# Weight units at other places within their SBUF slots, in a four-stage trunk on one core

## The chip, the core and the metric

The kernel runs on one core of one Trainium2 chip. What counts is the time on the device, in microseconds: the median of several runs of the whole kernel. Beside it stands one profiled execution, from which all durations of single instructions come.

## What is computed

One layer pair of a diffusion backbone, over 512 latent tokens and 256 context tokens of width 1024. Layer 0 is a hybrid mixer (neighbourhood attention beside spatial gating), layer 1 a retention in both directions; each is followed by a gated MLP with a depthwise convolution of width 3. Norms, and shifts, scales and gates made from a conditioning vector, lie around every part. Cut to what the change touches:

```python
q, k, v, u, g = jnp.split(h_lat @ w_in, splits, axis=-1)        # layer 0, hybrid
...
q, k, v, g = jnp.split(h_lat @ w_in, splits, axis=-1)           # layer 1, retention
kc, vc = jnp.split(h_ctx @ w_in[:, RET_QK_WIDTH:2 * RET_QK_WIDTH + RET_V_WIDTH], [RET_QK_WIDTH], axis=-1)
...
def conv_ffn(h, w_in, conv_w, conv_b, w_out):                   # both layers, D_FF = 2816
    a = dwconv3(h @ w_in, conv_w, conv_b)
    gate, up = jnp.split(a, 2, axis=-1)
    return (jax.nn.silu(gate) * up) @ w_out
```

## The kernel before

**Numbers in two parts.** Every product is made of float32 matrices that are split into a high part, rounded to the matmul's type fp32r, and the rest. `split` (lines 171 and 172) makes the high part on ScalarE and the rest on VectorE. `mm3` (lines 216 to 218) then needs three matmuls: high times high, high times low, low times high. `product` (whose calls show up as line 215 where they accumulate onto an open group) runs twelve of them over four slices of 128.

**Weight units.** Weights come in units of 128 x 1024 floats: a load into a ring of three raw tiles (`raw_unit`), then the split into a slot that holds both parts. `place` (line 185 on) gives slot `w0` to `w2` from the pool that lasts the whole kernel, and `w3` upward from the pool of a stage. A slot is either 2048 words wide, exactly two parts, or SLOT = 2112 words, 64 more. In the wide ones the two parts begin at word `at`, and `at` is any number up to 64:

```python
return [t[:, at + 1024 * x : at + 1024 * x + 1024] for x in range(2)]
```

64 words are 256 bytes. In the built program all wide slots, and the activations that meet them in matmuls (`h0`, `h1`, `hb`, `hs` and `blk`), begin at a multiple of 256 bytes, so `at` alone says how far a unit's start is from such a multiple. The high and the low part of a unit have the same remainder, since they are 4096 bytes apart.

**Which operand is which.** A matmul has one operand that is loaded into the array ahead (128 columns) and one that moves past it (256, 384 or 512 columns here). In the attention's projections (`project_pair`: wq, wk, wv), in the retention's queries and keys (`qk`: rwq, rwk) and in both MLPs' up-projections (wa, wb, wc, wd) the weights are loaded and the activations move. In the retention's values and gates (`nat`: rwv, rwg) the weights move and the activations are loaded.

**Places before.** The constants are Q1 = 16 and Q3 = 48 words. Attention projections, retention queries and keys lie at 0; values and gates at Q3; the MLPs' units at Q1, in the function `slot` of `ffn`. The second MLP's two further slots `w3` and `w4` are 2048 words wide and get their offset from gaps in the list of the stage's tiles (`order`, line 1511): 16 words ahead of `w3`, and 48 + 16 more ahead of `w4`, whose start is so also 16 words past a multiple of 64. The spatial gating's units, the output projections and the down-projections have places of their own, which stay.

**Stages.** `sgu` and `attention` (layer 0's mixer), `ffn(0)`, `retention`, `ffn(1)`. In the MLPs the hidden width is walked in 22 blocks of 128. The first two are made plainly; for the other twenty a scheme that saves products forms sums of halves of the weights and of the activations: units wa (rows 11 and 12), wb (s2, s3), wc (q3, q4) and wd (22), the last in a place of its own. A ring hands out the slots: `w2`, `w0`, `w1` in the first MLP, so wa is always in `w2`, wb in `w0`, wc in `w1`; `w0`, `w1`, `w3`, `w4` in the second, where three units per block rotate through four slots.

**Order.** The instructions of each engine stand in an order that is written out in a packed table (ORDER), which `queue` enforces. The DMA loads of weights are issued by the SP queue, each behind the one ahead of it.

Of the kernel before, what the change touches and what calls it, by code (L numbers as in the profile page):

```python
# [18 lines left out]
P = 128  # L19
# [16 lines left out]
EARLY = 2  # L36
SLOT = 2112
Q1, Q3 = 16, 48
MLP_PIECES = (
    ((0, (4, 5), 0, False), (0, (0,), 256, True), (1, (1,), 0, False), (1, (2,), 128, False), (1, (3,), 256, True)),  # L40
    ((0, (0,), 0, False), (0, (1,), 128, True), (1, (2,), 0, False), (1, (3,), 128, True)),
# [97 lines left out]
class Trunk:  # L139
# [563 lines left out]
    def finisher(self, gates, src, ab, name, xts, last=False, mlp=None):  # L703
# [23 lines left out]
        def third(r):  # L727
# [9 lines left out]
            else:  # L737
                for half, toks, c0, end in MLP_PIECES[mlp]:
                    if t in toks and all(u in done for u in toks):
# [239 lines left out]

    def project_pair(self, j, pr):  # L980

        w = [self.unit(self.a["hyb_qkv"][(4 * i + j) * P : (4 * i + j + 1) * P], f"w{'qkv'[i]}{j}") for i in range(3)]

        def lat(i):
            pr["qkv"[i]] = self.ps(f"p{'qkv'[i]}{j}", "A")
            self.proj_t(pr["qkv"[i]], w[i], 0)

        def con(i):
            if i == 0:
                pr["x"] = self.ps(f"px{j}", "A", (P, 2, 256))  # L990
            if i == 2:
                pr["y"] = self.ps(f"py{j}", "A")
            self.proj_t(pr["y"][:, :256] if i == 2 else pr["x"][:, i, :], w[i], 1)

        return [lambda f=f, i=i: f(i) for i in range(3) for f in (lat, con)]
# [177 lines left out]
    def retention(self, y, final):  # L1173
        S, V, T, G, a = self.S, self.V, self.T, self.G, self.a
        KS = float(np.float32(P) ** np.float32(-0.5))
        with ExitStack() as ctx:
            rp = self.phase(ctx, "retp", 3, SLOT)
            order = [("dist", ND), ("cos", 512), ("sin", 512), ("dec", 16), ("gng", 16), (None, 24)]
# [13 lines left out]
            gng = rp.tile([P, 16], F32, name="gng", tag="gng")  # L1192
            self.load(gng, a["gn_col"])
            w8 = lambda w: [x.rearrange("p (k c) -> p k c", k=4) for x in w]
            qk = lambda h, o, n: self.unit(a["ret_qk"][(o + h) * P : (o + h + 1) * P], f"rw{n}{h}")
            vg1 = lambda h, o, n, i, dst=None: w8(
                self.unit(a["ret_vg"][(o + h * 2 + i) * P : (o + h * 2 + i + 1) * P], f"rw{n}{h}{i}", dst, Q3)
            )
            vg = lambda h, o, n: [vg1(h, o, n, i) for i in range(2)]
            hd = [{} for _ in range(8)]  # L1200
# [180 lines left out]
            def gated(h):  # L1381
                d = hd[h]
                if h == 7:
                    gt = [x.rearrange("p (f c) -> p f c", f=2) for x in self.slot("gt7")]
                else:
                    gt = [rp.tile([P, 2, 512], F32R, name=f"gt{i}{h}", tag=f"gt{i}", bufs=1) for i in range(2)]
                for f in range(2):
                    pt = self.ps(f"rt{h}{f}", "A")
                    for t in range(4):
                        T.transpose(pt[:, t * P : (t + 1) * P], d["og"][t][:, f * P : (f + 1) * P], self.ident)  # L1390
                    gc = gng[:, 2 * h + f : 2 * h + f + 1]
                    S.activation(gt[0][:, f, :], pt, AF.Copy, scale=gc)
                    V.scalar_tensor_tensor(
                        out=gt[1][:, f, :],
                        in0=pt,
                        scalar=gc,
                        in1=gt[0][:, f, :].bitcast(F32),
                        op0=ALU.mult,
                        op1=ALU.subtract,
                    )  # L1400
                return [(gt[0][:, f, :], gt[1][:, f, :]) for f in range(2)]
# [6 lines left out]
            for h in range(8):  # L1408
# [35 lines left out]
                else:  # L1444
# [6 lines left out]
                    f = gated(h - 1)  # L1451
# [37 lines left out]
    def ffn(self, l, y, final, gates=None):  # L1489
# [4 lines left out]
        S, V, T, G, a = self.S, self.V, self.T, self.G, self.a  # L1494
        first = l == 0
        toks = (4, 5, 0, 1, 2, 3) if first else (0, 1, 2, 3)
        n = self.bn
        W = 770 if first else 512
# [4 lines left out]
        with ExitStack() as ctx:  # L1503
            fp = self.phase(ctx, f"ffnp{l}", 0)
            off = 62 if first else 0
            if first:
                order = [("blk", 9216), ("pre0", 2 * W), ("cv", 2 * W), ("cw", 176), ("yp", 1024)]
                order += [("g0", W + off, 3), ("g1", W + off, 3), ("rawu", 1024)]
            else:
                order = [("rawu", 1024), ("w5", 2048), ("w6", 2048), ("pre0", 1024), ("pre1", 1024), ("blk", 4096), ("cv", 1024)]  # L1510
                order += [(None, 16), ("w3", 2048), (None, 48), ("g0", W, 4), ("g1", W, 4), (None, 16), ("w4", 2048)]
                order += [("cw", 176), ("yp", 2048)]
            self.lay(fp, order)
            cw = fp.tile([P, 44, 4], F32, name=f"cw{l}", tag="cw")
# [11 lines left out]
                "o": ("y0", "y4", "y2") if first else ("w2", "w5", "w6"),  # L1526
            }

            def slot(kind, name, at=Q1):

                h = homes[kind][ring[kind] % len(homes[kind])]
                ring[kind] += 1
                if h == "fp":
                    return [fp.tile([P, 1024], F32R, name=f"{name}{x}", tag=tag) for x, tag in zip("hl", ("rawu", "yp"))]
                i = int(h[1])
                if h[0] == "w":
                    return self.place(i, name, at)
                pool = self.bp if i < 4 else self.lp
                return [pool.tile([P, 1024], F32R, name=f"{name}{x}", tag=f"y{i + m}", bufs=1) for m, x in enumerate("hl")]
# [63 lines left out]
            def weights(j):  # L1603
# [4 lines left out]
                def one():  # L1608
                    st["g"], st["u"] = win(j, 0), win(j, 1)
                    u = slot("i", f"wa{j}")  # L1610
                    self.split(u[0], u[1], st["g"])
                    d[11], d[12] = halves(u)

                def two():
                    u = slot("i", f"wb{j}")
                    g, up = st["g"], st["u"]
                    st["s"] = self.t2k(f"s2{j}"), self.t2k(f"s3{j}")
                    V.tensor_tensor(out=st["s"][0], in0=up[:, H[0]], in1=up[:, H[1]], op=ALU.subtract)
                    V.tensor_tensor(out=st["s"][1], in0=g[:, H[0]], in1=up[:, H[0]], op=ALU.subtract)
                    d["s", 2], d["s", 3] = halves(u)  # L1620
                    for x, v in zip((2, 3), st["s"]):
                        self.split(*d["s", x], v)
                    if soon:
                        up_half()

                def three():
                    u = slot("i", f"wc{j}")
                    q3, q4 = self.t2k(f"q3{j}"), self.t2k(f"q4{j}")
                    V.tensor_tensor(out=q3, in0=st["s"][0], in1=st["g"][:, H[0]], op=ALU.subtract)
                    V.tensor_tensor(out=q4, in0=q3, in1=st["g"][:, H[1]], op=ALU.add)  # L1630
                    d["q", 3], d["q", 4] = halves(u)
                    for x, v in ((3, q3), (4, q4)):
                        self.split(*d["q", x], v)
# [412 lines left out]
```

## Time and profile before

| what | value |
|---|---|
| median of 3 runs | 1786.02 us (1785.51 to 1786.25) |
| span of the profiled execution | 1784.0 us |
| instructions in it | 28774 |
| TensorE matmuls, and as many weight loads | 11024 |
| HBM read and written | 191.80 MB and 39.85 MB |
| DMA, mean over the span | 142 GB/s |

A row of the tables of the profile names a line of the kernel, an engine (PE is TensorE's matmuls, PEld its weight loads, DVE VectorE, ACT ScalarE, POOL GpSimd, SPq the SP queue), an operation, the tiles as output<-inputs without their numbers, and a shape. Matmuls overlap: the next starts before the last is through, so the length of one matmul is longer than the time from its start to the next start, and it is this time from start to start that adds up to the span.

### The profile page before, as it was taken

Reading aid. Unit: us, or ns where it says so; the run is one execution under the profiler, and the core shown is the slowest. Engines: PE = TensorE matmul, PEld = TensorE weight load, DVE = VectorE, ACT = ScalarE, POOL = GpSimd, SP = SyncE. Lnnn points to the kernel's source line nnn. Section 1 sums busy time; section 2 is a strip of 40 time slices with the busy share of each in tenths; the row PEclk is TensorE's granted clock in tenths of the full one; section 3 lists DMA queues with packets and bytes.
Section 4 is the critical chain, followed back from the end, with each engine's and each line's share of the span. In section 5 each row is a group of like instructions: output and inputs, shape, how many; then the busy total and the mean of one; then the engine's idle time right before and its main releaser. Section 6 shows DMA issues by size and latency. Waiting matters only on the chain.

```text
span 1784.0 us, 28774 instructions
## 1 busy us (share of the span) xinstructions
PE 1748.3 (98%) x11024; PEld 1578.7 (88%) x11024; DVE 1388.2 (78%) x2363; ACT 1017.5 (57%) x1882; POOL 340.1 (19%) x462
## 2 busy tenths in 40 slices
PE   7999999999999999999999999999999999999997
PEld 4898888799998999999899998998999789999996
DVE  3887886898887787889867666666655799998887
ACT  6633567776555555655665434433444577766773
POOL 1101322230132322222221001101001200222221
PEclk9999999999999999999999999999999999999999
DMA  8345331364687877886734332332322235887764
GB/s 304 116 133 165 99 110 45 106 180 118 171 174 174 173 174 155 164 178 161 257 126 125 118 113 71 119 95 81 97 71 60 107 122 147 214 216 185 180 145 130
DMA packets 84398, 253.44 MB, mean 142 GB/s; under 512 B 11026, under 2 KB 11538, under 8 KB 84260
## 3 DMA queue, kind: packets, MB, share of 16 engines
q1 hardware_dynamic: 55044, 191.27, 33.7%
q0 software_dynamic: 26912, 51.95, 17.1%
q10 hardware_dynamic: 2304, 8.39, 1.2%
q8 instruction: 86, 1.41, 0.3%
q14 instruction: 52, 0.43, 0.1%
HBM read 191.80 MB, written 39.85 MB: 130 GB/s over the span
## 4 chain that ended last, share of the span: by engine, by line
PE 89%; DVE 5%; ACT 3%; DMA 1%; issue 1%; POOL 1%; SPq 0%; DVEq 0%; POOLq 0%; ACTq 0%
PE px L215 11%; PE wf L216 4%; PE wf L217 4%; PE wf L218 4%; PE rn L217 4%; PE rn L216 4%; PE rn L218 4%; PE py L215 4%; PE px L216 2%; PE px L217 2%; PE px L218 2%; PE py L218 1%; PE py L217 1%; PE py L216 1%; PE ug L216 1%; PE ug L217 1%
## 5 line engine op out<-in xcount | busy, mean ns | idle before, releaser
L326 DVE SCALAR_TENSOR_TENSOR acc<-ar,cs,acc 128x512 f32<-128x512 f32 x256 | 190.5, 758 | 11.1 <-DMA ar<-in_adaw 4.3
L216 PE MATMUL rn<-rwv,h0c 128*128 128x256 f32 x384 | 107.8, 281 | 0.0
L217 PE MATMUL rn<-rwv,h0c 128*128 128x256 f32 x384 | 107.5, 281 | 0.0
L218 PE MATMUL rn<-rwv,h1c 128*128 128x256 f32 x384 | 107.2, 280 | 0.0
L1734 POOL DMA_DIRECT2D yf<-yp x64 | 56.0, 963 | 265.1 <-ACT yp L1730 237.7
L1574 ACT ACTIVATE pre<-px 128x256 f32<-128x256 f32 (+2 forms) x160 | 56.0, 369 | 78.0 <-PE px L215 55.9
L1587 DVE SCALAR_TENSOR_TENSOR cv<-pre,cw,cv 128x769 f32<-128x769 f32 (+1 forms) x88 | 77.3, 882 | 27.5 <-ACT cv L1586 26.9
L1586 ACT ACTIVATE cv<-pre,cw 128x770 f32<-128x770 f32 (+1 forms) x88 | 80.9, 925 | 21.5 <-DVE g L172 11.4
L1730 ACT COPY yp<-wf 128x512 f32<-128x512 f32 x118 | 68.4, 584 | 41.8 <-PE wf L218 34.2
L215 PE MATMUL px<-blk,wb 128*128 128x384 f32 (+1 forms) x480 | 79.2, 309 | 1.1 <-ACT pre L1574 1.1
L215 PE MATMUL px<-hs,wc 128*128 128x384 f32 (+1 forms) x480 | 78.9, 309 | 1.0 <-ACT pre L1574 0.8
L1590 DVE SCALAR_TENSOR_TENSOR cv<-pre,cw,cv 128x769 f32<-128x769 f32 (+1 forms) x88 | 76.8, 881 | 0.9
L215 PEld LDWEIGHTS px<-hs,wc 128*128 128x128 f32 x480 | 73.5, 188 | 4.1 <-ACT pre L1574 1.6
L215 PEld LDWEIGHTS px<-blk,wb 128*128 128x128 f32 x480 | 72.8, 188 | 3.8 <-ACT pre L1574 1.6
L171 ACT ACTIVATE wc<-q 128x512 fp32r<-128x512 f32 x80 | 49.8, 629 | 44.1 <-PE py L215 20.7
L216 PEld LDWEIGHTS rn<-rwv,h0c 128*128 128x128 f32 x384 | 72.4, 189 | 1.2 <-issue 0.2
L218 PEld LDWEIGHTS rn<-rwv,h1c 128*128 128x128 f32 x384 | 72.5, 189 | 0.7
L217 PEld LDWEIGHTS rn<-rwv,h0c 128*128 128x128 f32 x384 | 72.4, 188 | 0.9
L1734 POOL DMA_DIRECT2D yd<-ypg x48 | 48.4, 1053 | 122.1 <-ACT ypg L1730 104.6
L218 PE MATMUL rn<-rwg,h1c 128*128 128x256 f32 x256 | 71.3, 279 | 0.0
L217 PE MATMUL rn<-rwg,h0c 128*128 128x256 f32 x256 | 71.1, 279 | 0.0
L216 PE MATMUL rn<-rwg,h0c 128*128 128x256 f32 x256 | 71.1, 279 | 0.0
(1545 smaller groups left out, 6328.4 us busy)
## 6 DMA issues: line engine op xcount, KB each, us to landing
ar<-in_adaw SPq DMA_DIRECT2D x96, 512.0 KB
yf<-yp POOLq DMA_DIRECT2D x64, 256.0 KB, 4.3
yd<-yp POOLq DMA_DIRECT2D x54, 256.0 KB, 5.5
yd<-ypg POOLq DMA_DIRECT2D x54, 256.0 KB, 5.5
fin<-xd SPq DMA_DIRECT2D x8, 512.0 KB
xn<-in_x SPq DMA_DIRECT2D x6, 512.0 KB
xb<-in_x SPq DMA_DIRECT2D x6, 512.0 KB
xd<-xb ACTq DMA_DIRECT2D x6, 512.0 KB
```

The lines of the kernel that those rows point to most:

```text
L171: self.S.activation(hi, src, AF.Copy)
L215: mm = lambda *p, **k: self.T.matmul(*p, skip_group_check=True, **k)
L216: mm(out, lhs[0], rhs[0], start=first, stop=False)
L217: mm(out, lhs[0], rhs[1], start=False, stop=False)
L218: mm(out, lhs[1], rhs[0], start=False, stop=last)
L326: V.scalar_tensor_tensor(out=acc[s], in0=raw[:, kk * 512 : kk * 512 + 512], scalar=self.cs[:, 8 * s + k : 8 * s + k + 1], in1=acc[s], op0= ...
L1574: S.activation(pre[:, i, c : c + w], ps[:, b : b + w], AF.Copy, scale=scale)
L1586: S.activation(d, s, AF.Identity, scale=w1, bias=b)
L1587: V.scalar_tensor_tensor(out=d[:, 1:W], in0=s[:, 0 : W - 1], scalar=w0, in1=d[:, 1:W], op0=ALU.mult, op1=ALU.add)
L1590: V.scalar_tensor_tensor(out=d[:, 0 : W - 1], in0=s[:, 1:W], scalar=w2, in1=d[:, 0 : W - 1], op0=ALU.mult, op1=ALU.add)
L1730: S.copy(v, ps)
L1734: G.dma_start((yd[t] if first else y[t])[:, o], v, accum_op=ALU.add)
```

## The change

Four places get new numbers, and nothing else is edited. The attention's projections go from 0 to 32 words; the retention's keys from 0 to 48 (queries stay at 0), its values from 48 to 32 and its gates from 48 to 16; the first MLP's units from 16 to 32 (`w2`), 48 (`w0`) and 8 (`w1`); the second MLP's from 16 to 8 (`w0`), 24 (`w1`), 40 (`w3`) and 56 (`w4`). The units that the hooks of the stage before load ahead keep their places: the first head's two value units and its key unit, and the plain blocks' units wp.

```diff
 Q1, Q3 = 16, 48
+QK = {"q": 0, "k": 48}
+VG = {"v": 32, "g": 16}
+IN = {"w2": 32, "w0": 48, "w1": 8}, {"w0": 8, "w1": 24}
...
-        w = [self.unit(self.a["hyb_qkv"][(4 * i + j) * P : (4 * i + j + 1) * P], f"w{'qkv'[i]}{j}") for i in range(3)]
+        w = [self.unit(self.a["hyb_qkv"][(4 * i + j) * P : (4 * i + j + 1) * P], f"w{'qkv'[i]}{j}", at=32) for i in range(3)]
...
-            qk = lambda h, o, n: self.unit(a["ret_qk"][(o + h) * P : (o + h + 1) * P], f"rw{n}{h}")
+            qk = lambda h, o, n: self.unit(a["ret_qk"][(o + h) * P : (o + h + 1) * P], f"rw{n}{h}", at=QK[n])
             vg1 = lambda h, o, n, i, dst=None: w8(
-                self.unit(a["ret_vg"][(o + h * 2 + i) * P : (o + h * 2 + i + 1) * P], f"rw{n}{h}{i}", dst, Q3)
+                self.unit(a["ret_vg"][(o + h * 2 + i) * P : (o + h * 2 + i + 1) * P], f"rw{n}{h}{i}", dst, VG[n])
             )
...
-                order += [(None, 16), ("w3", 2048), (None, 48), ("g0", W, 4), ("g1", W, 4), (None, 16), ("w4", 2048)]
+                order += [(None, 40), ("w3", 2048), (None, 24), ("g0", W, 4), ("g1", W, 4), (None, 56), ("w4", 2048)]
                 order += [("cw", 176), ("yp", 2048)]
...
-            def slot(kind, name, at=Q1):
+            def slot(kind, name, at=None):
...
                 i = int(h[1])
+                if at is None:
+                    at = IN[l].get(h, Q1) if kind == "i" else Q1
                 if h[0] == "w":
                     return self.place(i, name, at)
```

In the built program 5616 of the matmuls get an operand at another remainder of 256 bytes. By how they stand to each other (moving operand's remainder, then the loaded one's, in bytes):

| matmuls | count | columns | before | now |
|---|---|---|---|---|
| attention wq, wk, wv | 288 and 288 | 512 and 256 | 0, 0 | 0, 128 |
| retention rwk, heads 1 to 7 | 168 and 168 | 512 and 256 | 0, 0 | 0, 192 |
| retention rwv, heads 1 to 7 | 1008 | 256 | 192, 0 | 128, 0 |
| retention rwg | 768 | 256 | 192, 0 | 64, 0 |
| first MLP wa, wb, wc | 480 each | 384 | 0, 64 | 0, 128; 0, 192; 0, 32 |
| second MLP wa, wb, wc | 1440, a quarter in each slot | 256 | 0, 64 | 0, 32; 0, 96; 0, 160; 0, 224 |
| second MLP, last down-projection units | 48 | 512 | 64, 0 | 160, 0 and 224, 0 |

In the second MLP's pool `w3` starts 96 bytes later, and `w4`, `cw` (the convolution's taps) and `yp` 160 bytes later; all other tiles stay.

The order of instructions on every engine is the same before and after. One wait is new, on the SP queue at the start of the second MLP, where the taps are loaded between units of the up-projection (f1..r) and of the down-projection (fo..r). Before:

```order
L157 DMA f102r<-in_ffn_in 128x1024 [waits DVE_49]
L157 DMA f112r<-in_ffn_in 128x1024 [waits DMAHW6_49,Pool_49]
L157 DMA cw_14737<-in_conv_col 128x176
L157 DMA f103r<-in_ffn_in 128x1024 [waits DMAHW1_49,DMAHW0_49,DVE_49]
L157 DMA fo10r<-in_ffn_out 128x1024 [waits DMAHW2_49,DVE_49]
```

And now (line 160 is the line 157 of before):

```order
L160 DMA f102r<-in_ffn_in 128x1024 [waits DVE_49]
L160 DMA f112r<-in_ffn_in 128x1024 [waits DMAHW6_49,Pool_49]
L160 DMA cw_14737<-in_conv_col 128x176 [waits PE_49]
L160 DMA f103r<-in_ffn_in 128x1024 [waits DMAHW1_49,DMAHW0_49,DVE_49]
L160 DMA fo10r<-in_ffn_out 128x1024 [waits DMAHW2_49,DVE_49]
```

The place is the same; the load of the taps now waits for TensorE, since its new bytes overlap the retention's tile `gt0`, whose last reader is the last matmul of that stage's output projection for head 6 (tile gt, number 06).

## Prediction

> **What bounds the kernel now.** First the page: busy shares, the granted clock and the shares of the chain that ended last.
>
> ```profile
> PE 1748.3 (98%) x11024; PEld 1578.7 (88%) x11024; DVE 1388.2 (78%) x2363; ACT 1017.5 (57%) x1882; POOL 340.1 (19%) x462
> PEclk9999999999999999999999999999999999999999
> PE 89%; DVE 5%; ACT 3%; DMA 1%; issue 1%; POOL 1%; SPq 0%; DVEq 0%; POOLq 0%; ACTq 0%
> ```
>
> TensorE is busy 98% of the span at an almost full clock, and 89% of the chain runs through it. Next the span by stage: input and attention, first MLP, retention, second MLP.
>
> ```profile
> 40.00:372.00 332.00, 327.14 (x2070) 276.97 (x2069) 269.03 (x591) 197.08 (x438) 71.80 (x105) 1.00 0.37 116
> 372.00:895.00 523.00, 518.53 (x2704) 476.67 (x2703) 437.96 (x630) 316.87 (x568) 127.08 (x169) 1.00 0.73 175
> 895.00:1425.00 530.00, 526.72 (x3706) 488.26 (x3704) 349.17 (x618) 239.10 (x385) 67.68 (x90) 1.00 0.32 98
> 1425.00:1765.00 340.00, 336.83 (x2372) 314.09 (x2371) 305.24 (x479) 235.62 (x428) 60.96 (x73) 0.99 0.66 169
> ```
>
> After each stage's length stand the busy times of PE, its weight loads, DVE, ACT and POOL. PE is idle 3 to 5 us in each of these four stages, so the kernel is a queue of matmuls, and its time is their number by the time from one start to the next. A nanosecond on each of a thousand matmuls is a microsecond of the kernel. The change touches just that: where the operands of matmuls lie, and nothing else.
>
> **What a place costs before.** Call "distance" the start of the moving operand minus that of the loaded (stationary) one, modulo 256 bytes. The head's key weights lie at distance 0 from the activations, the value and gate weights (48 words, 192 bytes) at 192, and the MLPs' weight units (16 words) at 192 too, one step of 64 bytes from 0 on the circle. The shape 128x256 occurs at both distances:
>
> ```profile
> L216 PEld LDWEIGHTS rkc<-h0c,rwk x64: 187/192/193, 903.0 to 1344.8; 128*128 128x128 f32 x64
> L216 PE MATMUL rkc<-h0c,rwk x64: 278/283/365, 903.0 to 1344.9; 128*128 128x256 f32 x64
> L216 PE MATMUL rn<-rwv,h0c x384: 276/281/369, 896.0 to 1376.1; 128*128 128x256 f32 x192
> L216 PE MATMUL rn<-rwg,h0c x256: 276/277/288, 916.8 to 1396.9; 128*128 128x256 f32 x128
> ```
>
> The three numbers are least, median and greatest length in ns. At distance 0 (rkc) a matmul takes 283 at the median, at 192 it takes 281 (values) or 277 (gates), with 276 as the least. The starts show what lies behind it: the first and the last row of a stretch of 24 key matmuls, of 18 value matmuls, and of 43 gate matmuls.
>
> ```profile
> 951.87 0.28 PE L216 MATMUL rkc<-h0c,rwk 128*128 128x256 f32 x1
> ...
> 954.63 0.28 PE L218 MATMUL rkc<-h0c,rwk 128*128 128x256 f32 x1
> 1123.89 0.28 PE L216 MATMUL rn<-rwv,h0c 128*128 128x256 f32 x1
> ...
> 1125.81 0.28 PE L218 MATMUL rn<-rwv,h1c 128*128 128x256 f32 x1
> 1129.72 0.28 PE L216 MATMUL rn<-rwg,h0c 128*128 128x256 f32 x1
> ...
> 1134.66 0.28 PE L216 MATMUL rn<-rwg,h0c 128*128 128x256 f32 x1
> ```
>
> Start to start that is 2.76/23 = 120 ns, 1.92/17 = 113 ns and 4.94/42 = 118 ns. So there are steady rhythms: a slow one that holds throughout at distance 0, and at distance 192 a short and a middle one, of which a stretch keeps the one it has fallen into. A length is the rhythm plus about 163 ns (283 and 120, 281 and 118, 276 and 113), so lengths can be used for prices.
>
> **The change, part by part.** No instruction is added, removed or moved; the 5616 matmuls below get another distance. Means by shape, last number but one of a row:
>
> ```profile
> L216 PE MATMUL rn<-rwv,h0c 128*128 128x256 f32 x384 | 107.8, 281 | 0.0
> L218 PE MATMUL rn<-rwv,h1c 128*128 128x256 f32 x384 | 107.2, 280 | 0.0
> L216 PE MATMUL rn<-rwg,h0c 128*128 128x256 f32 x256 | 71.1, 279 | 0.0
> L216 PE MATMUL rkc<-h0c,rwk 128*128 128x256 f32 x64 | 18.2, 284 | 0.0
> L216 PE MATMUL px<-h0a,wk 128*128 128x256 f32 x32 | 9.2, 286 | 0.0
> L217 PE MATMUL px<-h1a,wk 128*128 128x256 f32 x32 | 9.1, 285 | 0.0
> L216 PE MATMUL px<-hb,wa 128*128 128x256 f32 x80 | 22.4, 280 | 0.0
> L216 PE MATMUL pz<-hb,wa 128*128 128x384 f32 x80 | 26.9, 337 | 0.0
> L215 PE MATMUL px<-hs,wd 128*128 128x384 f32 x240 | 47.0, 337 | 0.0
> L217 PE MATMUL rk<-h1c,rwk 128*128 128x512 f32 x56 | 21.9, 390 | 0.0
> L216 PE MATMUL wf<-fo,g 128*128 128x512 f32 x144 | 56.8, 395 | 1.0 <-ACT pre L1574 1.0
> L217 PE MATMUL pz<-hb,wa x80: 331/336/340, 396.0 to 847.5; 128*128 128x384 f32 x80
> L215 PE MATMUL px<-hs,wd x240: 331/334/443, 418.0 to 859.0; 128*128 128x384 f32 x120
> ```
>
> The trace has distances 0 and 192 in numbers, but not 128, and no odd multiple of 32 bytes, so each term is bounded by its shape's short rhythm below and its slow one above. I take a simple scheme: 256-wide matmuls lose about 3.5 ns per step of 64 bytes away from 0 on the circle (284 at none, 280 at one, 276 to 277 at two). It rests on two points and is extended to a third.
>
> - Values: 7 heads (the first head's units stay), 6 tiles, 8 slices, 3 passes: 1008, from one step to two (192 to 128). I take 281 to 277: -4.0 us. Bounds: -4.7 (all 276) to +2.8 (all 283.5).
> - Gates: 8 x 4 x 8 x 3 = 768, from 192 to 64, one step on the other side: 0. Bounds -2.3 (279 to 276) to +3.5 (to 283.5).
> - Keys (7 heads) and attention projections (4 pairs, 3 units), 256-wide: 168 + 288 = 456, from 0 to one and two steps. I take -4 ns: -1.8 us; bounds 0 to -3.6 (284 to 276).
> - The same units 512-wide: 168 + 288 = 456, now at 390 to 395 by the nearest rows. Their shortest is 389, so there is little to win; I take +1.5 ns, 0.7 us; bounds -0.5 to +2.3 (all at the wf row's 395).
> - First MLP, 128x384: 20 blocks x 72 = 1440, a third each at steps two (unit a), one (b) and a half (c). The rows show no trend here: wd lies at distance 0 and has the same mean of 337 as wa at 192, and even the lower median, 334 against 336. I take 0; bounds -4.3 (to 334) to +3.7 (to 339.6, near the greatest of the row with least, median and greatest).
> - Second MLP, 128x256: 1440, a quarter in each slot, at distances 224, 160, 96 and 32: half of them half a step nearer to 0 than before, half of them half a step farther. By the scheme +1.3 and -1.3, so 0; bounds -5.0 (280 to 276) to +5.8 (to 284). The 48 down-projection matmuls in these slots count for nothing.
>
> Sum -4.0 - 1.8 + 0.7 = -5.1 us. All lower bounds together give -20.4, all upper ones +18.1.
>
> What I cost at nothing: the ScalarE and VectorE splits that fill the moved units, since the two places seen before cost the same (rwk at 0, rwv at 192):
>
> ```profile
> L171 ACT ACTIVATE rwk<-rwk1r x1: 1051/1051/1051, 947.7 to 947.7; 128x1024 fp32r<-128x1024 f32 x1
> L172 DVE TENSOR_TENSOR rwk<-rwk1r,rwk x1: 1215/1215/1215, 949.6 to 949.6; 128x1024 fp32r<-128x1024 f32 x1
> L171 ACT ACTIVATE rwv<-rwv10r x1: 1063/1063/1063, 965.8 to 965.8; 128x1024 fp32r<-128x1024 f32 x1
> L172 DVE TENSOR_TENSOR rwv<-rwv10r,rwv x1: 1225/1225/1225, 966.8 to 966.8; 128x1024 fp32r<-128x1024 f32 x1
> ```
>
> And the one new wait: the second MLP's load of cw now waits for the retention's last read of gt, since cw has moved 160 bytes.
>
> ```profile
> 1418.85 0.39 PE L218 MATMUL wrC<-rwo,gt 128*128 128x512 f32 x1
> 1430.05 0.52 SPq L157 DMA_DIRECT2D cw<-in_conv_col  x1
> 1432.92 0.33 SPq L157 DMA_DIRECT2D f103r<-in_ffn_in  x1
> ```
>
> The last such matmul is over at 1419.24, and SP comes to that load at 1430.05: 10.8 us of slack. Were it gone, f103r and the loads of the down-projection behind it on SP would be late by what is missing.
>
> The sum is made against the profiled execution, whose span is 1784.0 us; the runs have a median of 1786.02, 2.0 above it. Taken off the median: 1786.0 - 5.1 = **1780.9 us**.
>
> **A rule against it.** By the rows above, the key matmuls at distance 0 are some 4 ns longer than the gates at 192 in the same stage and shape, so place matters at least at 0. The Trainium skill ("TensorE: Matmul & The Clock Gate", "Step-by-step: what each phase is for") says that PE has two independent SBUF read ports and that loading the next weights takes no read bandwidth from the running matmul. By that rule place would cost nothing and the sum would be 0; the trace speaks against it at distance 0, and cannot say whether it holds among the other distances.
>
> **The rivals.**
>
> 1. *Only exact coincidence counts, or nothing does.* Then every distance but 0 is alike, and only the 456 narrow key and attention matmuls gain: 1786.0 - 1.8 = 1784.2; if place has no effect, 1786.0. For it: gates and values share one distance and still differ by 2 ns, so what a stretch fell into weighs as much as where it lies. Against it: the sharp step at 0, which makes one more step away worth something. Both times are within 0.2%. This is also how it looks if the change does not do what it says.
> 2. *Odd multiples of 32 bytes bind (slower).* All four slots of the second MLP, and slot w1 of the first, then hold weights that start half-way into a 64-byte step. If such a start clashes like distance 0 does, all of them go to the slow rhythm. Price: 1440 x 4 ns + 480 x 2.6 ns = 5.8 + 1.2 us, less the 1.8 of the narrow ones: +5.2, so 1791.2. It decides from 2.8 ns a matmul upward: (3.6 + 1.8)/1920. For it: no such place is in the trace, and the only ones there are whole steps. Against it: nothing in the rows but that the 384-wide shape hardly feels place.
> 3. *The short rhythm nearly everywhere.* If distance 0 is the only place that pulls a stretch out of it, and the moved units start clear of it, most of the lower bound comes in: three quarters of -20.4, so 1770.7. For it: stretches at 113 ns last over 18 matmuls and more once begun. Against it: at 192 the middle rhythm lasts as long.
>
> **How the numbers follow.** Forecast 0.40, rival 1 0.25, rival 2 0.22, rival 3 0.13. A measurement of this kernel can tell about 0.2% from no change, 3.6 us: the bounds are 1782.4 and 1789.6. Forecast and rival 3 lie below, 0.53; rival 1 is the same, 0.25; rival 2 is above, 0.22. The two signs hold most of the chance together, so the range reaches from a little below rival 3 to rival 2's time: 1769 to 1791.5. The forecast's own range is 1776 to 1782.4.
>
> **What would show it.** In the changed kernel the value matmuls should have a median of 277 or less, where it was 281; the key and attention matmuls 128x256 one of 281 or less, where it was 283; the second MLP's slots should divide, with units in w1 and w3 below 280 and those in w0 and w4 above. PE's idle time by stage and the cw load's time should stay as they are, and the splits' 1.05 and 1.22 us too. The prediction is wrong if values at 128 are no shorter than at 192, if the 512-wide key and attention matmuls rise by more than 5 ns, or if the second MLP moves as one block: up means rival 2, down rival 3. If lengths stay and the time changes, the cause is not in the matmuls at all.

## The result, and the profile after

The changed kernel takes 1792.1 us at the median of 7 runs (1791.32 to 1793.49); the kernel before, run beside it, 1786.37 us (1785.51 to 1788.3). The ratio is 1.0033, with a 95% interval of 1.0022 to 1.0044: slower by 0.33%, where the prediction said 0.3% faster, and 0.6 us above the upper end of its range.

From the page of the changed kernel, its span, the busy times and the granted clock:

```profile
span 1790.3 us, 28774 instructions
PE 1754.0 (98%) x11024; PEld 1582.5 (88%) x11024; DVE 1389.0 (78%) x2363; ACT 1017.8 (57%) x1882; POOL 339.0 (19%) x462
PEclk9999999999999999999999999999999999999999
```

The span is 6.3 us longer than before. PE's busy time went up by 5.7 us (1748.3 to 1754.0), with as many matmuls at nearly the same mean granted clock (0.997 before, 0.996 now); what is left of the span, PE's idle time, went from 35.7 to 36.3 us. DVE, ACT and POOL moved by 1.1 us or less. So the loss lies where the prediction looked, in the time from one matmul to the next, but with the other sign.

First the wait that was costed at nothing. These are the end of the retention's output projection on PE and SP's load of the taps, in the timeline of the changed kernel (start in us, length in us):

```profile
1422.54 0.39 PE L221 MATMUL wrC<-rwo,gt 128*128 128x512 f32 x1
1433.74 0.53 SPq L160 DMA_DIRECT2D cw<-in_conv_col  x1
1436.62 0.33 SPq L160 DMA_DIRECT2D f103r<-in_ffn_in  x1
```

The last reader of gt ends at 1422.93, 10.8 us ahead of the load, and f103r follows the load by 2.88 us, where it was 2.87. The new wait is always over when SP comes to it.

Now a stretch of 39 value matmuls, the same ones in both programs; its first and last row in the kernel before (distance 192 bytes) and in the changed one (128):

```profile
1050.15 0.28 PE L218 MATMUL rn<-rwv,h1c 128*128 128x256 f32 x1
...
1054.47 0.28 PE L217 MATMUL rn<-rwv,h0c 128*128 128x256 f32 x1
```

```profile
1051.75 0.28 PE L221 MATMUL rn<-rwv,h1c 128*128 128x256 f32 x1
...
1056.31 0.28 PE L220 MATMUL rn<-rwv,h0c 128*128 128x256 f32 x1
```

Start to start that is 4.32/38 = 113.7 ns before and 4.56/38 = 120.0 ns now. This stretch held the short rhythm before, so its loss is larger than the average one. The length in each row is 0.28 us in both. Single lengths and medians tell little, as the view of one tile shows (least, median, greatest ns); values first, then gates, then unit wa of the second MLP in the changed kernel:

```profile
L219 PE MATMUL rn<-rwv,h0c x384: 274/281/369, 896.6 to 1379.5; 128*128 128x256 f32 x192
L221 PE MATMUL rn<-rwv,h1c x384: 274/282/290, 897.0 to 1379.7; 128*128 128x256 f32 x192
L219 PE MATMUL rn<-rwg,h0c x256: 276/279/285, 917.4 to 1400.5; 128*128 128x256 f32 x128
L219 PE MATMUL px<-hb,wa x80: 277/280/286, 1454.5 to 1748.2; 128*128 128x256 f32 x80
```

The values' median is 281 or 282, against 281 before, although they lost 2 ns from start to start. Their mean length does show it, 282 to 283 in the changed kernel where the prediction's rows had 280 and 281:

```profile
L219 PE MATMUL rn<-rwv,h0c 128*128 128x256 f32 x384 | 108.4, 283 | 0.0
L221 PE MATMUL rn<-rwv,h1c 128*128 128x256 f32 x384 | 108.1, 282 | 0.0
```

What adds up to the span is the starts. Setting every matmul's time to the next start beside that of the same matmul in the other trace, and adding up by group, gives:

| group | count | mean before, now (ns) | measured | predicted |
|---|---|---|---|---|
| values | 1008 | 117.5, 119.6 | +2.1 us | -4.0 |
| gates | 768 | 116.1, 116.9 | +0.6 | 0 |
| keys and attention, 256 wide | 456 | keys 120.3, 118.0 | -0.5 | -1.8 |
| the same, 512 wide | 456 | wq 243.9, 248.0; keys 229.0, 230.5 | +1.1 | +0.7 |
| first MLP, wa, wb, wc | 1440 | wa 177.6, 178.3; wb 176.0, 174.5 | -0.7 | 0 |
| second MLP, wa, wb, wc, and the 48 down-projection matmuls | 1488 | wa 118.7, 120.6; wb 119.3, 121.0; wc 118.9, 119.8 | +2.3 (wa, wb, wc alone +2.2) | 0 |
| all matmuls that were not moved | 5408 | | +1.2 | 0 |

The moved groups make +4.9 of the span's +6.3 us.

### The profile page after: what moved, and what is told of

The parts are those of the page before. It is cut to its first block, busy times and chain, and to the rows that moved or that the text cites. A ratio compares the mean times of both kernels' runs of the same rounds, so it can differ in the third digit from the quotient of the medians.

```text
span 1790.3 us, 28774 instructions
## 1 busy us (share of the span) xinstructions
PE 1754.0 (98%) x11024; PEld 1582.5 (88%) x11024; DVE 1389.0 (78%) x2363; ACT 1017.8 (57%) x1882; POOL 339.0 (19%) x462
## 4 chain that ended last, share of the span: by engine, by line
PE 89%; DVE 5%; ACT 2%; DMA 1%; issue 1%; POOL 1%; SPq 0%; DVEq 0%; POOLq 0%; ACTq 0%
PE px L218 11%; PE wf L219 5%; PE wf L221 5%; PE wf L220 5%; PE rn L220 4%; PE rn L221 4%; PE rn L219 4%; PE py L218 4%; PE px L221 2%; PE px L219 2%; PE px L220 2%; PE py L221 1%; PE py L220 1%; PE py L219 1%; PE ug L219 1%; PE pz L221 1%
## 5 line engine op out<-in xcount | busy, mean ns | idle before, releaser
L1739 POOL DMA_DIRECT2D yd<-ypg x48 | 48.2, 1050 | 119.4 <-ACT ypg L1735 101.9
```

The source lines that it names most:

```text
L1739: G.dma_start((yd[t] if first else y[t])[:, o], v, accum_op=ALU.add)
```

## Experiments

Theory A: the place of the two operands alone sets the rhythm, by a rough map that the prediction's scheme does not describe. Theory B: the rhythm comes from work beside the matmuls, or from which units stand next to each other.

**A map of places without the kernel.** m1_map leaves out the whole network. It holds nothing but loads, copies and streams of matmuls, each stream with one place (cut):

```python
for x in range(48):
    k = x % 8
    nc.tensor.matmul(
        ps[:, :n],
        sta[:, s + 128 * k : s + 128 * k + 128],
        mov[:, m + n * k : m + n * k + n],
        ...
```

`mov` and `sta` begin at one remainder of 256 bytes; m and s are the words past it.

> Nothing of the trunk is computed: TensorE alone runs streams of 48 matmuls, one stream for each place of the moving operand (0 to 62 words past the loaded one) and each width (256, 384, 512), twice, with no other engine at work inside a stream. Theory A (the distance of the two operands sets the rhythm on TensorE itself): 256 columns: 120 ns from start to start at distance 0, 113 or 118 at 16 and 48 words, 119 at 32 words and never 113 there; 512 columns: 227 at 0 and 233 at 32 words; pairs with the same distance but both moved (32 and 32) as distance 0. Theory B (places matter only through the writes of ScalarE, VectorE or DMA that go on beside the matmuls): every stream of one width has the same rhythm.

In the timeline of m1_map each stream of 48 is one row (start, length of the whole stream; the tile's name holds m). Second pass, moving operand at word 0, 16 and 32, and the loaded one at 0; then both at 32:

```profile
158.71 6.01 PE L82 MATMUL ps2561m0s<-mov,sta 128*128 128x256 f32 x48 [0.52 <-DVE res L89]
190.97 5.71 PE L82 MATMUL ps2561m16s<-mov,sta 128*128 128x256 f32 x48 [0.52 <-DVE res L89]
216.56 5.96 PE L82 MATMUL ps2561m32s<-mov,sta 128*128 128x256 f32 x48 [0.52 <-DVE res L89]
293.92 6.01 PE L82 MATMUL ps2561m32s<-mov,sta 128*128 128x256 f32 x48 [0.52 <-DVE res L89]
```

Sixteen words shorten the stream by 0.30 us, 6.4 ns a matmul, while no other engine works. The steady rhythms behind the rows, means over the later starts of a stream, are 120.0, 113.3 and 118.6 ns, and 120.0 again with both at 32. In the first pass word 16 gave 117.8. So theory A holds as far as this: with nothing beside the matmuls, place alone moves the rhythm, at these places only the distance counts, and some places leave two rhythms open. 128 bytes, which the prediction took for the best place of all, is a slow one.

**Every distance.** m2_map moves the moving operand through words 0 to 63, m3_map the loaded one.

> Nothing of the trunk is computed: streams of 40 matmuls on TensorE alone, one for every distance from 0 to 63 words, 256 columns twice, 384 and 512 columns once, and for each width two streams in which the places alternate from matmul to matmul: one with distance 28 words between the operands of each matmul (and 56 or 0 to the loaded operand of the following one), one the other way round. Theory A: a rough landscape that repeats the coarse map: 112 to 114 ns at 28 words, 118 to 120 at 0, 20, 24, 32; 512 columns 227 at 0 and 28 alone or nearly. Theory A1 (a matmul meets the load of the following one): the alternating stream with 28 towards the following load is at 113 ns and 227, the other at 116 to 120 and 231 to 235. Theory A2 (what counts is the place within one matmul): the other way round. Theory C (what matters is only whether places are multiples of 64 bytes): 28 is then as slow as 20 and 36.

> Leaves out the whole network: TensorE streams of 40 matmuls as in m2_map, but with the moving operand at word 0 and the loaded one at word 0 to 63 (widths 256 twice, 384, 512), so the same distances from the other side; then one stream with the moving operand at word 36 and one with the loaded at 28. Theory D (the distance alone decides): the loaded operand at word d repeats what the moving one gave at word 64-d: 256-wide 113.3 ns at words 36 and 16, 512-wide 228.9 at 48 and 231 at 36; then the slow second MLP of b1_moved28, with its units at word 36, has another cause. Theory E (each operand's own start counts below 64 bytes): only the multiples of 16 words repeat the other side (16: 113.3 or 117.8, 32: 118.6, 48: 117.8), and word 36 gives 118.5 ns or more at 256 and 233 or more at 512; 8, 24, 40 and 56 (the four places of the changed second MLP) give 118.5 to 120 ns, with 40 and 24 no better than 8.

Steady rhythms in ns at the multiples of 32 bytes, for 256, 384 and 512 columns, by the starts in the two traces:

| distance, bytes | moving operand shifted | loaded operand shifted |
|---|---|---|
| 0 | 120.0, 173.3, 226.7 | 120.0, 173.3, 226.7 |
| 32 | 116.7, 173.3, 233.3 | 116.7, 173.4, 233.4 |
| 64 | 117.8, 173.3, 228.9 | 117.8, 173.3, 228.9 |
| 96 | 120.0, 176.7, 233.3 | 120.1, 176.6, 233.3 |
| 128 | 118.7, 175.6, 232.4 | 118.7, 175.6, 232.4 |
| 160 | 117.3, 173.3, 234.4 | 117.3, 173.3, 234.4 |
| 192 | 113.3, 176.6, 233.3 | 117.8 and 113.3, 174.7, 233.2 |
| 224 | 118.4, 173.3, 233.3 | 118.4, 173.3, 233.4 |

Of the streams 256 wide, those at 64 and 192 bytes fall into one of two rhythms, 113.3 or 117.8 (in m1_map both distances gave both). The table's other values are not all fixed either: m1_map also has 117.8 ns at 32 bytes in its first pass, and for 384 columns 173.3 and 176.7 at 32 and at 192 bytes. There is no slope from 0 to 128 bytes. The best place for 512 columns (0) is among the worst of these eight for 256.

Away from the multiples of 32 bytes the two sides part: 256 wide, the moving operand at word 28 gives 113.3 and the loaded one at word 36, the same distance, 116.7; the moving operand at words 1, 5, 9 and so on up to 61 gives 120 to 123.4. Theory C of m2_map falls, since word 28 is not as slow as words 20 and 36 (118.3 and 118.8). Its theory A had 227 ns for 512 columns at word 28: m1_map has 226.7 there, m2_map 231.1. Theory D of m3_map falls away from the multiples of 32 bytes and holds at them, and theory E is wrong where it puts the turn at 64 bytes and gives word 36 at least 118.5 ns. Two more streams of m2_map asked whether the distance of 28 words counts within a matmul or between a moving operand and the next loaded one: 116.8 ns for the first, 118.9 for the second. Neither took the 113.3 of the plain stream, so that stays open.

**The change in three parts.**

e1_values moves the values alone, e2_mlp2 the second MLP's four slots alone, e3_rest all else. Their edits, against before, before, and the changed kernel (lines that only repeat the places of before are left out):

```diff
+VG = {"v": 32, "g": 48}
```

```diff
+IN = {"w2": 16, "w0": 16, "w1": 16}, {"w0": 8, "w1": 24}
-                order += [(None, 16), ("w3", 2048), (None, 48), ("g0", W, 4), ("g1", W, 4), (None, 16), ("w4", 2048)]
+                order += [(None, 40), ("w3", 2048), (None, 24), ("g0", W, 4), ("g1", W, 4), (None, 56), ("w4", 2048)]
```

```diff
-VG = {"v": 32, "g": 16}
-IN = {"w2": 32, "w0": 48, "w1": 8}, {"w0": 8, "w1": 24}
+VG = {"v": 48, "g": 16}
+IN = {"w2": 32, "w0": 48, "w1": 8}, {"w0": 16, "w1": 16}
-                order += [(None, 40), ("w3", 2048), (None, 24), ("g0", W, 4), ("g1", W, 4), (None, 56), ("w4", 2048)]
+                order += [(None, 16), ("w3", 2048), (None, 48), ("g0", W, 4), ("g1", W, 4), (None, 16), ("w4", 2048)]
```

> The kernel before with the value weights alone at word 32 (distance 128 bytes). Theory A: the value matmuls rise from 117.5 to 119.6 ns from start to start as in the changed kernel, 1008 of them, so +2.1 us, and no value stretch keeps 113 ns; all other groups stay. Theory B: what rises is not tied to the values; time and value matmuls as before, 1786.4 us.

> The kernel before with the second MLP alone changed (words 8, 24, 40, 56, with its new gaps and the new wait of cw). Theory A: +2 us in that MLP, all of it in the matmuls on the moved units (116.8 to 118.5 ns), spread over the slots, with the slots at distances 96 and 160 worst; nothing else moves. Rival (the shifted tiles behind the gaps or the new wait of the cw load cost the time): +2 us too, but as idle time of TensorE at the start of that MLP, or in groups whose operands did not move.

> The changed kernel with values and second MLP put back; attention projections, keys, gates and the first MLP stay changed. Theory A: the sum of what these groups showed in the changed kernel: gates +0.6, keys -0.1, attention +0.7, first MLP -0.7, so +0.5 us, 1786.9. Rival (the whole is more than its parts, by when transfers or waits fall): over +2 us, or under -2.

| part | median, us | ratio, 95% interval | its moved groups |
|---|---|---|---|
| e1_values | 1788.72 | 1.0016 (1.0006 to 1.0026) | values +2.2 us |
| e2_mlp2 | 1789.09 | 1.0013 (1.0004 to 1.0023) | second MLP +2.2 |
| e3_rest | 1787.82 | 1.0010 (1.0001 to 1.0020) | retention +0.7, attention +0.6, first MLP -0.5 |

The moved groups of the three parts add up to +5.2 us, against +4.9 in the changed kernel, and the three excesses to 0.39%, against 0.33% (within the intervals). So no sign is seen that the parts need or hinder each other. In e1_values the values go from 117.5 to 119.7 ns, and every other group that the change moves stays within 0.4 us.

By the medians (1785.78 for the kernel before) each part lost more than its moved groups: 2.9, 3.3 and 2.0 us against 2.2, 2.2 and 0.8. For e3_rest +0.5 was expected. In its trace and in that of e1_values the granted clock is at half (0.50) for 10.2 us at the start of the second MLP, in before and in the changed kernel for 6.8 us. The matmuls around it, none of them moved, take 0.8 to 0.9 us more than before in those two traces. What is left of the three excesses is not explained.

**The worst place for a whole stage.** If the map holds in the kernel, it must also say which place makes the kernel slower still. d1_mlp2_40 puts all four slots of the second MLP at word 40, 96 bytes.

```diff
+IN = {}, {"w0": 40, "w1": 40}
-                order += [(None, 16), ("w3", 2048), (None, 48), ("g0", W, 4), ("g1", W, 4), (None, 16), ("w4", 2048)]
+                order += [(None, 40), ("w3", 2048), (None, 24), ("g0", W, 4), ("g1", W, 4), (None, 40), ("w4", 2048)]
```

> Kernel before, with all four slots of the second MLP at word 40 (distance 96 bytes, where the maps show 120.0 ns, the slowest of the eight multiples of 32 bytes), and nothing else moved. If the map of places sets the rhythm in the kernel too: its units go from a mix of 113 and 118 to a steady 119 to 120 ns, 1440 x 3.5 to 4 ns = +5.0 to +5.8 us, ratio 1.003. If what a slot costs depends on the slot or on the unit that it holds and not on the place alone: about +2.3 us, as when the four slots lay at four places, ratio 1.0013.

1791.13 us, ratio 1.0025 (1.0015 to 1.0034). The units lost 4.8 us, twice what they lost in the change, at almost the size that was expected from the map (5.0 to 5.8). The values, which were not moved here, took 0.4 us less than before: of 82 blocks of nine successive matmuls without a pause between, 22 ran at 113 ns, where 13 had. So the share of stretches in the short rhythm changed between two traces with the same place, and a group at such a place is known only to about this much. 24 matmuls of unit wc, two timeline rows of twelve each, first in the kernel before, then in d1_mlp2_40:

```profile
1733.89 1.58 PE L215 MATMUL px<-hs,wc 128*128 128x256 f32 x12
1735.31 1.58 PE L215 MATMUL py<-hb,wc 128*128 128x256 f32 x12
```

```profile
1737.73 1.60 PE L218 MATMUL px<-hs,wc 128*128 128x256 f32 x12
1739.17 1.59 PE L218 MATMUL py<-hb,wc 128*128 128x256 f32 x12
```

Twelve starts take 1.42 us before (118 ns) and 1.44 us at 96 bytes (120 ns). In the changed kernel these matmuls lie in slot w3, also at 96 bytes, and do the same:

```profile
1740.09 1.60 PE L218 MATMUL px<-hs,wc 128*128 128x256 f32 x12
1741.53 1.59 PE L218 MATMUL py<-hb,wc 128*128 128x256 f32 x12
```

**Better places.** b1_moved28 puts every moved matmul at a distance of 28 words, the one place but 48 where m2_map has 113.3: values and gates at word 28, loaded units at word 36. b2_wide28 adds the first head's units, the queries, the gating units and the MLPs' plain units. From b1_moved28's edit:

```diff
+QK = {"q": 0, "k": 36}
+VG = {"v": 28, "g": 28}
+IN = {"w2": 36, "w0": 36, "w1": 36}, {"w0": 36, "w1": 36}
...
+                if h in ("w3", "w4"):
+                    at = 36 if kind == "i" and at else 0
+                    t = fp.tile([P, SLOT], F32R, name=name, tag=h, bufs=1)
+                    return [t[:, at + 1024 * x : at + 1024 * x + 1024] for x in range(2)]
```

> The matmuls that the change moved, all at a distance of 28 words (values and gates at word 28; keys, attention projections and both MLPs' units at word 36, with w3 and w4 widened instead of gaps). Theory A (the map holds inside the kernel): 256 columns at 113 to 115 ns: values -3 to -4 us, gates -2, second MLP -4 to -5, narrow keys and attention -2 to -3; 384 columns at 173 to 174: -1.5 to -2.5; in all -12 to -16 us, 1770 to 1774. Rival (interruptions every 12 matmuls reset the rhythm, so the place hardly shows): -4 us or less, 1782 or more.

> As b1_moved28, and also the units that the change left at their places: the first head's values and key, the queries, the plain blocks' units, and the spatial gating's second half of units. Theory A: another 144 values, 216 gating matmuls, 72 keys and some 300 of the plain blocks at 4 ns each, -2 to -3 us beyond b1_moved28, 1768 to 1772. Rival: no further gain, since these stretches are short or wait for other engines.

Both were slower, 1.0018 (1.0009 to 1.0027) and 1.0025 (1.0016 to 1.0034), where 12 us and more had been expected as a gain. In b1_moved28 the half in which the moving operand was shifted gained (values -1.5 us, gates -0.7), the half with the loaded one at word 36 lost: second MLP +3.4, attention +0.8, and the keys 512 wide went from 229.0 to 234.4 ns, having left distance 0, the best place for that width. This is what sent m3_map after the other side.

c1_moved28_mlp48 keeps what had gained: values and gates at word 28, the first MLP's three slots at word 48 (64 bytes), the rest as before. c2_mlp2_19 adds the second MLP's four slots at word 19, where m3_map shows 113.3 in both passes. From c2_mlp2_19's edit:

```diff
+QK = {"q": 0, "k": 0}
+VG = {"v": 28, "g": 28}
+IN = {"w2": 48, "w0": 48, "w1": 48}, {"w0": 19, "w1": 19}
...
+                    at = 19 if kind == "i" and at else 0
```

> Kernel before, with values and gates at word 28 and the first MLP's three slots at word 48 (distance 64 bytes); keys, queries, attention and second MLP as before. If the gains seen one by one stand alone: values -1.5, gates -0.66, first MLP 1440 x -1.5 ns = -2.2, together -4.3 us, ratio 0.9976. If 64 bytes was only good for the one unit that lay there (128x384 is nearly flat): -2 to -2.5 us, ratio 0.9987.

> As c1_moved28_mlp48, and all four slots of the second MLP at word 19, where m3_map shows 113.3 ns in both passes. If the map of single streams carries over to the kernel below 32 bytes: the units go from 116 to 113.5 ns, 1440 x -2.2 = -3.2 us more, ratio 0.996. If it carries over only at multiples of 32 bytes (word 36 was 116.7 in the map and 120 in the kernel): 117 to 120 ns, 0 to +6 us more, ratio 0.998 to 1.001.

c1_moved28_mlp48 takes 1782.96 us, ratio 0.9985 (0.9976 to 0.9994). By its time alone it is nearer to the smaller gain of the two expected; but its moved groups gain what the larger one was made of, values -1.6, gates -0.7, first MLP -2.3 us, and matmuls that were not moved gave back 1.3 us of it. c2_mlp2_19 takes 1780.01 us, ratio **0.9962** (0.9950 to 0.9974), faster than both kernels of the change. The second MLP's units gained 2.5 us, of 3.2 expected. Its page, its values, and the 24 wc matmuls from above:

```profile
PE 1740.4 (98%) x11024; PEld 1570.3 (88%) x11024; DVE 1388.8 (78%) x2363; ACT 1016.9 (57%) x1882; POOL 339.8 (19%) x462
```

```profile
L219 PE MATMUL rn<-rwv,h0c x384: 275/275/369, 895.4 to 1374.1; 128*128 128x256 f32 x192
L219 PE MATMUL px<-hb,wa x80: 276/276/285, 1447.9 to 1736.8; 128*128 128x256 f32 x80
```

```profile
1728.86 1.54 PE L218 MATMUL px<-hs,wc 128*128 128x256 f32 x12
1730.24 1.56 PE L218 MATMUL py<-hb,wc 128*128 128x256 f32 x12
```

PE is busy 7.9 us less than before. Twelve starts take 1.38 us, 115 ns, and the median lengths have fallen to the least ones (275, 276).

**Why word 36 was slow.** The map gave 116.7 ns for the loaded operand at word 36, the kernel 119.4 in its steady stretches. m4_order asks whether the kernel's sequence makes the difference: two matmuls with the high part of a weight slice, then one with its low part.

```python
k, y = (x // 3 % 8, x % 3) if three else (x % 8, 0)
m = 256 * k + (2048 if y == 1 else 0)
t = s + 128 * k + (1024 if y == 2 else 0)
```

> Leaves out the whole network: TensorE streams of 48 matmuls 128x256 with the moving operand at word 0 and the loaded one at words 0, 8, 16, 19, 24, 32, 36, 40, 48, 56, each three times; first with the slices in plain sequence as in m3_map, then in the kernel's sequence of three (high and high, high and low, low and high of one slice, the low parts 4096 and 8192 bytes on). Theory F (below 32 bytes the sequence of slices counts too): both sequences agree at the multiples of 8 words (120.0 at 0 and 40, 116.7 at 56, 117.4 at 24, 118.4 at 8, 118.7 at 32), and at word 36 the plain one gives 116.7 as in m3_map, the kernel's 119 to 120 as in b1_moved28. Theory G (something outside TensorE made word 36 slow in the kernel, or the pieces around it): 116.7 at word 36 in both. Word 19 should give 113.3 in both by either, since the kernel with it ran at 113.5; 16 and 48 should take 113.3 or 117.8.

The second pass of the kernel's sequence in m4_order's timeline; the loaded operand at words 0, 0, 8, 16, 19, 24, 32, 36, 40, 48 and 56, one row each:

```profile
299.57 6.02 PE L81 MATMUL ps1r1q<-mov,sta 128*128 128x256 f32 x48 [0.52 <-DVE res L84]
306.11 6.01 PE L81 MATMUL ps1r1q<-mov,sta 128*128 128x256 f32 x48 [0.52 <-DVE res L84]
312.63 5.94 PE L81 MATMUL ps1r1q<-mov,sta 128*128 128x256 f32 x48 [0.52 <-DVE res L84]
319.08 5.72 PE L81 MATMUL ps1r1q<-mov,sta 128*128 128x256 f32 x48 [0.52 <-DVE res L84]
325.32 5.72 PE L81 MATMUL ps1r1q<-mov,sta 128*128 128x256 f32 x48 [0.52 <-DVE res L84]
331.55 5.90 PE L81 MATMUL ps1r1q<-mov,sta 128*128 128x256 f32 x48 [0.52 <-DVE res L84]
337.97 5.96 PE L81 MATMUL ps1r1q<-mov,sta 128*128 128x256 f32 x48 [0.52 <-DVE res L84]
344.44 5.87 PE L81 MATMUL ps1r1q<-mov,sta 128*128 128x256 f32 x48 [0.52 <-DVE res L84]
350.83 6.02 PE L81 MATMUL ps1r1q<-mov,sta 128*128 128x256 f32 x48 [0.52 <-DVE res L84]
357.37 5.71 PE L81 MATMUL ps1r1q<-mov,sta 128*128 128x256 f32 x48 [0.52 <-DVE res L84]
363.60 5.87 PE L81 MATMUL ps1r1q<-mov,sta 128*128 128x256 f32 x48 [0.52 <-DVE res L84]
```

The map can be read off this column: 6.02 at word 0 and at word 40, 5.72 at 16 and 19. The steady rhythms are those of the plain sequence: 120.0, 118.3, 113.3, 113.3, 117.3, 118.6, 116.7 (word 36) and 120.1 in every pass of both, apart from the very first stream; 48 gave 117.8 five times and 113.4 once, 56 gave 116.7 to 117.8. Theory F falls: this sequence does not matter, and word 36 is not slow in either. Theory G is left, that something else in the kernel made it slow; what, no run shows.

## Why the prediction was wrong

**What held.** The kernel is a queue of matmuls, place sets the time from one to the next, and the change does nothing else: the cw load has the same slack as before, and DVE and ACT, on which the splits run, have the same busy times to 0.8 us. Each measured group also lies within the bounds that the prediction gave it; what was wrong is the point that it chose between them. Of its signs, the narrow keys and attention matmuls came to medians of 279 and 281 ns, from 283, and the 512-wide ones rose by no more than 5 ns; but the values did not get shorter.

**The step that failed** is the scheme "256-wide matmuls lose about 3.5 ns per step of 64 bytes away from 0 on the circle", as applied to *Values: from one step to two*. It read two distances as a slope and extended it to a third. The runs show no slope but a map. Next to the map stand the steady rhythms of the kernels themselves (means over blocks of nine matmuls, from the starts in the traces of before and after):

| distance, bytes | map, 256 wide | in the kernels | where |
|---|---|---|---|
| 0 | 120.0 | 119.9 | keys, before |
| 192 | 113.3 and 117.8 | 116.1 | values and gates, before |
| 192 | 113.3 and 117.8 | 116.7 | second MLP, before |
| 128 | 118.7 | 119.3 | values, after |
| 64 | 117.8 and 113.3 | 116.4 | gates, after |
| 32 | 116.7 | 116.7 | second MLP, w4 |
| 96 | 120.0 | 119.9 | second MLP, w3 |
| 160 | 117.3 | 118.4 | second MLP, w1 |
| 224 | 118.4 | 118.3 | second MLP, w0 |

The values left one of the two places in this table where the short rhythm occurs, and went to one that never has it. Of the 82 blocks of nine value matmuls, 13 ran at 113 ns and 57 at 118 in the kernel before; in the changed kernel, and in e1_values, none is below 117. The term *Values* measured +2.1 us in place of -4.0, 6.1 of the 11 us between the forecast and the result.

**Second MLP, 0 by the scheme.** The criterion was that units in w1 and w3 fall below 280 ns and those in w0 and w4 rise above. The slots did divide, but otherwise: w3 is the slowest, w4 the fastest. The scheme's halves do not cancel because 192 bytes was already one of the two best of the eight places: the mean of the four new ones by the map, 118.1 (from 120.0, 117.3, 118.4 and 116.7), is 1.4 ns above the 116.7 of before, so +2.0 us; measured +2.2, shown alone in e2_mlp2 and doubled in d1_mlp2_40. The 48 down-projection matmuls, which the prediction left out, made 0.1.

**The small terms.** Narrow keys and attention gained 0.5 instead of 1.8 us, as only the keys went to a place with two rhythms, and the attention to 118.7. The 512-wide ones lost 1.1 instead of 0.7 us: right in sign, since distance 0 is best for that shape (226.7 against 228.9 and 232.4). Gates at +0.6 against 0 fit a place with the same two rhythms. First MLP -0.7 against 0: the rows' "no trend" hid differences that the map has, 173.3 at 64 and 224 bytes and 175.6 at 128.

**The rivals.** Rival 2's time, 1791.2, was only 0.9 us off, but by luck. It priced the second MLP at +5.8 us, slot w1 of the first at +1.2 and the values at nothing; measured were +2.2, -0.4 (unit wc) and +2.1. Of the odd multiples of 32 bytes only 96 is as slow as distance 0 (120.0 ns); 32, 160 and 224 have 116.7, 117.3 and 118.4, and the values lost at 128, an even one. Rival 1 falls with the same table, since distances other than 0 differ by up to 6.7 ns, and rival 3 because the places moved to lack the short rhythm or hold it only in part.

**Pricing by lengths.** The error did not come from there. The prediction's sum used mean lengths, and its "plus about 163 ns" held: for the moved values, mean length less mean time from start to start is 162.8 ns before (280.3 and 117.5) and 162.9 now (282.5 and 119.6). Medians are the poorer guide. In d1_mlp2_40 the units' median lengths are 281 to 282, as before, while their starts are 2.5 to 4.3 ns further apart, group by group, and their mean lengths 1.4 to 2.3 ns longer.

**The rule against it.** By the Trainium skill ("TensorE: Matmul & The Clock Gate", "Step-by-step: what each phase is for") loading the next weights takes no read bandwidth from the running matmul. Taken as "place costs nothing", that does not agree with m1_map, where place alone made 113.3 or 120.0 ns. What part of the chip the two operands meet in, no run here shows.

**What stays open.** Why the loaded operand at word 36 runs at 116.7 ns in streams and 119.4 in the kernel, what decides which of the two rhythms a stretch at 64 or 192 bytes falls into, and where the matmuls that were not moved got their +1.2 us. The stretch at half clock is not the answer there, since it lasts 6.8 us both before and now.

## What to carry to other kernels

Two measured places are not a slope: before moving operands, time a stream of matmuls of the kernel's own shape and type at every candidate place, with nothing else running; run each stream more than once, since some places have two rhythms. At multiples of 32 bytes such a map held in the kernel to about 1 ns; between them it can fail by more (word 36: 116.7 and 119.4). Price matmuls that overlap by their starts, or by mean lengths, but not by medians. And choose the place for each width by itself, since the best one for 512 columns was among the worst for 256.

## What was unexpected of the hardware

- In this type, the start of the two operands within 256 bytes changes the time from start to start between 113.3 and 123.4 ns at 256 columns, 173.3 and 181 at 384, and 226.7 and 244 at 512, with no other engine at work.
- At multiples of 32 bytes only the difference counts, to 0.1 ns in most cases; below that, which of the two operands is shifted matters too.
- A stream 256 wide at 64 or 192 bytes held 113.3 or 117.8 ns, and could take the other one the next time it ran with the same operands.
